# Attention in fp32: unsplit scores on halves of the rows, exponential as stationary operand, normalised by query

## The chip, the cores and the metric

The kernel runs on 1 core of one Trainium2 chip. The metric is the device time of one execution in microseconds (us); lower is better. Before the change the median of 3 runs is 2341.67 us (2341.45 to 2349.15).

## The reference, cut to what matters

Two layers work on 512 tokens (256 of context, 256 latent). Each is a feed-forward half, three token mixers side by side (S5, attention, RWKV-7), a gated merge of the three, and another feed-forward half. Attention has 8 query heads of width 64 over 2 key/value heads (4 query heads to each). Latent queries see all 512 tokens, context queries only the 256 context tokens, and the second layer needs no context output.

```python
def attend(q, k, v):
    s = jnp.einsum('bqhgd,bkhd->bhgqk', q, k).astype(F32) * (HEAD_DIM ** -0.5)
    p = jax.nn.softmax(s, axis=-1).astype(v.dtype)
    return jnp.einsum('bhgqk,bkhd->bqhgd', p, v)
...
    def merge(gate_pre, ys5, yatt, yrw):
        g_s5, g_att, g_rw = jnp.split(jax.nn.sigmoid(gate_pre), N_BRANCH, axis=-1)
        mixed = g_s5 * (ys5 @ w_br_s5) + g_att * (yatt @ w_br_att) + g_rw * (yrw @ w_br_rwkv)
        return mixed @ w_out
```

## The kernel before, in words

Most products are fp32 made of three products in the reduced type fp32r: each operand is split into a high part (a copy by ACT, L932, L921) and a low part (a subtraction, mostly on DVE, L933, L922), and `mm3` (L937 to L939) multiplies high by high, high by low and low by high. In the function `mixers` one layer's dense projections come first; then a generator `attention` and the S5 mixer `s5_main` are woven, step by step, into the issue of the program while RWKV-7 runs its 8 loops (0 to 7 in the first layer, 8 to 15 in the second). The gate products (`pg`, L937 to L939, 256 columns each, their weights `ghpg` and `glpg`) belong to no chain; they fill PE between other work. Which instruction stands where in each engine's queue is decided by the scheduler when the kernel is built: every engine then works its list strictly in order. After S5's last products (`s5g`, L747, then `s5tg` L749 and `s5o` L750) the S5 output goes through DRAM (`yd`, then `er`) in the first layer, is split (`es`, L1374 on ACT, L1375 on DVE) and multiplied with the merge weights (`pb..e`, with `ee` as weights, added up into `eg`, L1386 on DVE); remaining gates stand among and behind them; then the attention part of the merge follows and the output projection `po`.

Class `Att` does attention in units of (tp, half): tp=0 is context (256 keys, nk=2 blocks of 128), tp=1 latent (512 keys, nk=4), half picks 128 queries of each head group. The first layer has four units, the second two (tp=1). `kv` (L818) loads keys and values, normalises, transposes keys on PE (`atk`) and writes them split: high parts `kh` (ACT, L833) and low parts `kl` (DVE, L835), each on both halves of the 128 partitions; values likewise (`vh` L824, `vl` L825), with 64 columns of ones between the two heads. `q` (L836) does the same for queries (`atqs`, L848 and L849): the high part of a head stands on one half of the partitions and the low part on the other, so that one product over 128 rows holds two of the four terms.

`core` (L850) then has three stages. **Scores** (`ats`, L862 and L863): two fp32r products per head and query group, 40 row maxima by DVE (L864). **Exponential**: the maxima are transposed (`atm`) and stand in `mT`; for each of the two heads and each key block the scores are made again, transposed (`atp`, L883 and L884), with a third product (L885) that takes the maxima off; ACT makes `atP` = exp (L887) and its high part `atph` (L889), DVE the low part `atpl` (L890). **Values** (`ato`, L892 to L894): three products with the values as stationary operand and 512 columns of exponentials moving; 64 of the 128 result rows are the output of one head, the other 64 are its sums of exponentials. ACT copies both out (L895, L897), DVE takes the reciprocal of 128x512 sums (L899) and multiplies (L900), and `att_out` (L1284) hands the output on: split into the merge's operands (L1288, L1289 in the second layer), or through DRAM for tp=0. PSUM tiles come from four tags of two buffers each; `px` holds scores and `ato`, `pa` holds `atp`, `atm`, `atk` and `atq`.

Of the kernel before, what the change touches and what calls it, by code (L numbers as in the profile page):

```python
# [769 lines left out]
class Att:  # L770


    def __init__(s,K,L,pool,last):
# [44 lines left out]
    def kv(s,tp,kd):  # L818

        K=s.K; nc=K.nc; L=s.L  # L820
        kw=s.T([128,2,256],"qw",K.ATB[3]); nc.sync.dma_start(kw,kd)
        for h in range(2):
            v=kw[:,:,128+h*64:192+h*64]; vh=s.vh[:,2*tp:2*tp+2,2*h]
            nc.scalar.activation(vh,v,AF.Copy)  # L824
            nc.vector.tensor_sub(s.vl[:,2*tp:2*tp+2,2*h],v,vh.bitcast(F32))  # L825
        kr=s.heads(tp,1,kw[:,:,0:128].rearrange("p t (h d) -> p t h d",h=2),2,f"k{tp}")
# [2 lines left out]
        pf=pk.rearrange("p t c -> p (t c)"); c=slice(tp*256,tp*256+256)
        for hh in range(2):  # L830
            R=slice(hh*64,hh*64+64)
            for P in (R,slice(64-hh*64,128-hh*64)):
                nc.scalar.activation(s.kh[P,hh,c],pf[R],AF.Copy)  # L833
            for P in (R,slice(64-hh*64,128-hh*64)):
                nc.vector.tensor_sub(s.kl[P,hh,c],pf[R],s.kh[R,hh,c].bitcast(F32))  # L835
    def q(s,tp,half,qd):  # L836

        K=s.K; nc=K.nc; L=s.L; T=s.T; nm=f"{tp}{half}"
        qw=T([128,2,256],"qw",K.ATB[3]); nc.sync.dma_start(qw,qd)
# [5 lines left out]
        qs=T([128,2,4,128],"qs",K.ATQ,F32R)  # L845
        for hh in range(2):
            R=slice(hh*64,hh*64+64); Q=slice(64-hh*64,128-hh*64)
            nc.scalar.activation(qs[R,hh],pt[R],AF.Copy)  # L848
            nc.vector.tensor_sub(qs[Q,hh],pt[R],qs[R,hh].bitcast(F32))  # L849
        return qs  # L850
    def core(s,tp,half,qs,yd):
# [5 lines left out]
        m=T([128,8],"m",2)  # L857
        for h in range(2):
            for g in range(0,4,r):
                ps=K.ats([128,r,n],f"ats{nm}{h}{g}")  # L860
                for i in range(r):
# [612 lines left out]
```

## Time and profile before

| what | value |
|---|---|
| median of 3 runs | 2341.67 us (2341.45 to 2349.15) |
| profiled execution, its own time | 2342.22 us |
| span of that execution, first to last instruction | 2340.4 us |
| mean granted TensorE clock | 0.963 |
| PE busy | 2200.1 us (94%) |
| DVE busy | 1610.6 us (69%) |
| ACT busy | 967.5 us (41%) |
| POOL busy | 581.3 us (25%) |

The span is cut by hand into stretches of time in the rows below. In such a table of windows each engine has its busy time and, in brackets, its number of instructions in the stretch; PEclk is the mean granted TensorE clock as a share of full speed (1.0 is 2.4 GHz, 0.5 is 1.2 GHz). An fp32 product that isn't of the reduced type shows as two records of equal length on PE. Ends of records on PE are modelled, so the distance from start to start says what a product costs.

### The profile page before, as it was taken

To read this page: it belongs to the slowest core of one execution; us is meant where nothing else is said; L and a number is where in the kernel's file an instruction comes from. 1 tells how busy PE (TensorE), PEld (TensorE's weight loads), DVE (VectorE), ACT (ScalarE), POOL (GpSimd) and SP (SyncE) were. 2 spreads that over 40 slices of the span, in tenths; PEclk is the share of its full clock that TensorE was granted. 3 is DMA by queue.
4 is the path that set the end of the run, shared out by engine and by line. 5 is a ranking of instruction groups with operands and counts; after the bars stand their busy time and mean duration, and the time that the engine had idled before them with its cause. 6 is when DMAs were issued, how large, how long until landed. Compare 5 with 4: busy or idle time off the path is not lost.

```text
span 2340.4 us, 40316 instructions
## 1 busy us (share of the span) xinstructions
PE 2200.1 (94%) x14562; PEld 1882.2 (80%) x14562; DVE 1610.6 (69%) x3195; ACT 967.5 (41%) x2002; POOL 581.3 (25%) x712
## 2 busy tenths in 40 slices
PE   8999888989989979899999999999998988989999
PEld 5888767868789848688888888888887877878999
DVE  4896898564887769577457575546656489877655
ACT  4333333344445442443233343324434444555554
POOL 0006663221444415400000001504103145431000
PEclk9999999989999979899999999999997979999999
DMA  7574665324343624545445436536513534455664
GB/s 277 184 227 147 206 223 181 124 76 159 103 122 109 212 73 135 177 140 174 132 142 180 130 112 214 187 121 201 189 55 108 160 97 128 139 179 192 178 188 131
DMA packets 222668, 363.42 MB, mean 155 GB/s; under 512 B 54018, under 2 KB 94082, under 8 KB 221316
## 3 DMA queue, kind: packets, MB, share of 16 engines
q1 hardware_dynamic: 220308, 360.09, 48.2%
q8 instruction: 114, 1.87, 0.3%
q10 hardware_dynamic: 2160, 0.76, 0.1%
q14 instruction: 86, 0.70, 0.1%
HBM read 320.90 MB, written 39.86 MB: 154 GB/s over the span
## 4 chain that ended last, share of the span: by engine, by line
PE 59%; DVE 9%; DMA 3%; issue 3%; POOL 2%; ACT 2%; SPq 1%; ACTq 0%; DVEq 0%; POOLq 0%
PE p L938 13%; PE p L937 13%; PE p L939 13%; PE pg L939 2%; PE pg L937 2%; PE pg L938 2%; PE it L208 1%; PE po L939 1%; PE po L937 1%; PE po L938 1%; DVE s5w L705 1%; PE s5y L722 1%; DMA wrq<-w_q 1%; DVE glpg L922 0%; PE pq L938 0%
## 5 line engine op out<-in xcount | busy, mean ns | idle before, releaser
L932 ACT ACTIVATE wh<-wr 128x512 fp32r<-128x512 f32 (+1 forms) x568 | 348.7, 619 | 689.6 <-PE p L938 606.4
L933 DVE TENSOR_TENSOR wl<-wr,wh 128x512 fp32r<-128x512 f32 (+1 forms) x568 | 411.6, 728 | 298.0 <-ACT wh L932 280.0
L938 PE MATMUL p<-hlo,wh 128*128 128x512 f32 (+1 forms) x1440 | 519.1, 361 | 1.5 <-DVE hlo L1124 0.9
L939 PE MATMUL p<-hhi,wl 128*128 128x512 f32 (+1 forms) x1440 | 518.3, 360 | 0.0
L937 PE MATMUL p<-hhi,wh 128*128 128x512 f32 (+1 forms) x1440 | 514.2, 362 | 2.6 <-ACT hhi L1077 1.5
L938 PEld LDWEIGHTS p<-hlo,wh 128*128 128x128 f32 x1440 | 274.1, 190 | 43.9 <-DVE hlo L1124 1.8
L937 PEld LDWEIGHTS p<-hhi,wh 128*128 128x128 f32 x1440 | 271.7, 190 | 45.0 <-ACT hhi L1077 1.6
L939 PEld LDWEIGHTS p<-hhi,wl 128*128 128x128 f32 x1440 | 274.1, 190 | 40.8 <-issue 0.6
L1007 DVE SCALAR_TENSOR_TENSOR s<-ad,cb 128x1024 f32<-128x1024 f32 x224 | 292.2, 1306 | 4.1 <-DMA ad<-w_ada 1.1
L937 PE MATMUL p<-ghi,wh 128*128 128x512 f32 (+1 forms) x704 | 248.9, 354 | 0.0
L939 PE MATMUL p<-ghi,wl 128*128 128x512 f32 (+1 forms) x704 | 248.5, 353 | 0.0
L938 PE MATMUL p<-glo,wh 128*128 128x512 f32 (+1 forms) x704 | 248.3, 353 | 0.0
L939 PE MATMUL pg<-hhi,glpg 128*128 128x256 f32 x512 | 154.3, 303 | 7.5 <-DVE glpg L922 5.2
L937 PE MATMUL pg<-hhi,ghpg 128*128 128x256 f32 x512 | 153.1, 299 | 2.2 <-ACT ghpg L921 2.2
L938 PE MATMUL pg<-hlo,ghpg 128*128 128x256 f32 x512 | 148.8, 291 | 0.0
L937 PEld LDWEIGHTS p<-ghi,wh 128*128 128x128 f32 x704 | 133.2, 189 | 18.7 <-issue 0.6
L939 PEld LDWEIGHTS p<-ghi,wl 128*128 128x128 f32 x704 | 133.1, 189 | 18.1
L938 PEld LDWEIGHTS p<-glo,wh 128*128 128x128 f32 x704 | 133.2, 189 | 17.7
L921 ACT ACTIVATE ghpg<-wrpg 128x256 fp32r<-128x256 f32 x176 | 72.7, 415 | 127.2 <-PE pg L938 108.3
L939 PEld LDWEIGHTS pg<-hhi,glpg 128*128 128x128 f32 x512 | 100.5, 197 | 18.8 <-DVE glpg L922 8.1
L1107 POOL TENSOR_TENSOR rsf<-msf,mhalf 128x2 f32<-128x2 f32 x5 | 3.6, 712 | 426.9 <-DVE msf L1106 426.9
L937 PEld LDWEIGHTS pg<-hhi,ghpg 128*128 128x128 f32 x512 | 101.3, 198 | 8.8 <-ACT ghpg L921 5.2
(724 smaller groups left out, 4244.7 us busy)
## 6 DMA issues: line engine op xcount, KB each, us to landing
wr<-w SPq DMA_DIRECT2D x480, 256.0 KB
ad<-w_ada SPq DMA_DIRECT2D x128, 512.0 KB
wrpg<-w_g SPq DMA_DIRECT2D x96, 256.0 KB
wr<-w SPq DMA_DIRECT2D x64, 192.0 KB
s5tab<-s5tabd SPq DMA_DIRECT2D x16, 640.0 KB
s5tabd<-s5tb SPq DMA_DIRECT2D x16, 384.0 KB
wrpf<-w_f SPq DMA_DIRECT2D x24, 256.0 KB
wrq<-w_q SPq DMA_DIRECT2D x24, 256.0 KB
```

The lines of the kernel that those rows point to most:

```text
L208: nc.tensor.matmul(pi[:,c,:],BK[R,c].rearrange("p j b -> p (j b)"),s.ZL[par][R,hf,dq,c,o],start=True,stop=True)
L705: V.tensor_tensor_scan(w[:,jj,c,1:129],m,a[:,jj,c,:],initial=0.0,op0=ALU.mult,op1=ALU.add)
L722: x=hv(St[d][:,jj,c]); nc.tensor.matmul(hv(py[:,jj]),CLs[d][:,c,jj,sl],x[:,:,::-1] if d else x,start=False,stop=(d==1 and c==1))
L921: K.nc.scalar.activation(hi,raw,AF.Copy)
L932: nc.scalar.activation(hi[:,0:n],raw,AF.Copy)
L933: (nc.gpsimd if eng=='pool' or i<=K.PW else nc.vector).tensor_sub(lo[:,0:n],raw,hi[:,0:n].bitcast(F32))
L937: nc.tensor.matmul(ps,lhi,rhi,start=start,stop=False)
L938: nc.tensor.matmul(ps,lhi,rlo,start=False,stop=False)
L939: return nc.tensor.matmul(ps,llo,rhi,start=False,stop=stop).ins
L1007: nc.vector.scalar_tensor_tensor(K.junk,raw,1.0,K.cb[:,v,:],op0=ALU.mult,op1=ALU.mult,accum_out=K.M[L][:,v,ct:ct+1])
L1107: nc.gpsimd.tensor_tensor(rs[:,r],ms[:,r],K.mhalf[:,0:2],op=ALU.pow)
```

## The change

Nothing is split in attention any more; its products are plain fp32.

- `kv` loads keys and values by three transfers per call instead of one, values straight into a tile `v` whose 65th column is one. One copy by ACT (`kT`) takes the place of four copies and four subtractions. `q` has one copy by ACT in place of two copies and two subtractions.
- Scores: one product per head and group over 64 rows, the two heads on opposite halves of the rows, written one after the other in the code; head 0 goes to PSUM tag `px`, head 1 to `pa`.
- Exponential: for each key block first the product with the maxima (`sel`, L864 of the new kernel), then one over 64 rows (L865). `atph` and `atpl` are gone.
- Values: four products per head and key block (L861), with 128x128 exponentials as stationary operand and 65 columns of values and ones moving. They stand a key block behind the scores. Queries are now on the partitions, so that the sums of exponentials are one column per group: reciprocals of 128x4 (L873), a multiplication of 128x4x64 per head (L874), and four transposes by PE per unit (`atz`, L876) to bring features back onto partitions.
- `attp` has 4 buffers in place of 1, `atto` 2 in place of 1. `att_out` reads the transposed tile from PSUM; for tp=0 ACT copies it out first (`atyz`).

```diff
-            nc.scalar.activation(vh,v,AF.Copy)
-            nc.vector.tensor_sub(s.vl[:,2*tp:2*tp+2,2*h],v,vh.bitcast(F32))
...
+        for t in range(2): nc.sync.dma_start(s.v[:,2*tp+t,:,0:64],kd[:,t,128:256].rearrange("p (h d) -> p h d",h=2))
...
-                nc.scalar.activation(s.kh[P,hh,c],pf[R],AF.Copy)
...
-                nc.vector.tensor_sub(s.kl[P,hh,c],pf[R],s.kh[R,hh,c].bitcast(F32))
+        nc.scalar.activation(s.kT[:,tp*256:tp*256+256],pk.rearrange("p t c -> p (t c)"),AF.Copy)
...
+        qs=T([128,4,128],"qs",K.ATQ)
+        nc.scalar.activation(qs,pt,AF.Copy)
...
-                    nc.tensor.matmul(ps[:,i],qs[:,h,g+i],s.kh[:,h,0:n],start=True,stop=False)
-                    s.mark=nc.tensor.matmul(ps[:,i],qs[:,h,g+i],s.kl[:,h,0:n],start=False,stop=True)
...
+            pp=[(K.px,K.pa)[h]([128,r,n],f"ats{nm}{h}{g}") for h in range(2)]
+            for i in range(r):
+                for h in range(2): nc.tensor.matmul(pp[h][:,i],qs[R[h],g+i],s.kT[R[h],0:n],start=True,stop=True)
+            for h in range(2): V.tensor_reduce(m[:,h*4+g:h*4+g+r],pp[h],axis=AX.X,op=ALU.max,negate=True)
...
+        po=[K.px([128,4,65],f"ato{nm}{h}") for h in range(2)]
+        def values(k,P):
+            for g in range(4):
+                for h in range(2): nc.tensor.matmul(po[h][:,g],P[h][:,g],s.v[:,k,h],start=k==0 and g==0,stop=k==nk-1 and g==3)
+        for k in range(nk):
+            pp=[K.pa([128,4,128],f"atp{nm}{h}{k}") for h in range(2)]
+            for h in range(2): nc.tensor.matmul(pp[h],s.sel[:,h:h+1].to_broadcast([128,128]),s.mT,start=True,stop=False)
+            for h in range(2): nc.tensor.matmul(pp[h],s.kT[R[h],k*128:k*128+128],qs[R[h]].rearrange("p g n -> p (g n)"),start=False,stop=True)
+            if k: values(k-1,P)
+            P=[s.tp([128,4,128],f"P{nm}{h}{k}") for h in range(2)]
+            for h in range(2): nc.scalar.activation(P[h],pp[h],AF.Exp)
+            if k==nk//2-1: yield
+        values(nk-1,P)
+        y=s.to([128,4,2,64],f"y{nm}"); rc=T([128,8],"rc",2)
         for h in range(2):
...
-                ps=K.pa([128,4,128],f"atp{nm}{h}{k}"); kc=slice(k*128,k*128+128)
-                qf=qs[:,h].rearrange("p g n -> p (g n)")
-                nc.tensor.matmul(ps,s.kh[:,h,kc],qf,start=True,stop=False)
-                nc.tensor.matmul(ps,s.kl[:,h,kc],qf,start=False,stop=False)
-                nc.tensor.matmul(ps,s.sel[:,h:h+1].to_broadcast([128,128]),s.mT,start=False,stop=True)
-                P=s.tp([128,4,128],f"P{nm}{h}{k}")
-                nc.scalar.activation(P,ps,AF.Exp)
-                ph=T([128,4,128],"ph",K.ATP[0],F32R); pl=T([128,4,128],"pl",K.ATP[1],F32R)
-                nc.scalar.activation(ph,P,AF.Copy)
-                V.tensor_sub(pl,P,ph.bitcast(F32))
-                vh=s.vh[:,k,h:h+2].rearrange("p a d -> p (a d)")
-                nc.tensor.matmul(po,vh,ph,start=k==0,stop=False)
-                nc.tensor.matmul(po,s.vl[:,k,h:h+2].rearrange("p a d -> p (a d)"),ph,start=False,stop=False)
-                nc.tensor.matmul(po,vh,pl,start=False,stop=k==nk-1)
-            nc.scalar.activation(y[R],po[R],AF.Copy)
-            if h==0: dn=s.tt([128,4,128],f"dn{nm}")
-            nc.scalar.activation(dn[R],po[O],AF.Copy)
-            if h==0: yield
-        for g in range(0,4,K.RG): V.reciprocal(dn[:,g:g+K.RG],dn[:,g:g+K.RG])
-        V.tensor_mul(y,y,dn)
-        yd(tp,half,y)
+            V.reciprocal(rc[:,h*4:h*4+4],po[h][:,:,64])
+            V.tensor_mul(y[:,:,h],po[h][:,:,0:64],rc[:,h*4:h*4+4].unsqueeze(2).to_broadcast([128,4,64]))
+        pt=K.pa([128,4,128],f"atz{nm}")
+        for g in range(4): nc.tensor.transpose(pt[:,g],y[:,g].rearrange("p h d -> p (h d)"),K.ident)
+        yd(tp,half,pt)
```

The scheduler makes every engine's list anew, and the change moves much in `mixers` that it doesn't name. Below, a row is the line, the operation, result and operands by their names (the digits of `atp`, `ato` and `ats` are layer, tp, half, head, and key block or group), the shape that moves, and a count.

PE, first layer, unit tp=1, half=0, first and second key block, before:

```order
L885 MATMUL atp01000_7504<-atmT0_6877,atsel0_6882 128x512
L883 MATMUL atp01001_7517<-atqs0_7246,atkh0_6870 128x512
L884 MATMUL atp01001_7517<-atqs0_7246,atkl0_6871 128x512
L885 MATMUL atp01001_7517<-atmT0_6877,atsel0_6882 128x512
L939 MATMUL pg09_9172<-hhi_86,glpg094_9210 128x256
```

The same place now (L913 to L915 is `mm3` in the new kernel, L323 and L343 belong to RWKV):

```order
L913 MATMUL pg021_8536<-hhi_86,ghpg0214_8573 128x256
L864 MATMUL atp01001_7435<-atmT0_6876,atsel0_6879 128x512
L865 MATMUL atp01001_7435<-atqs0_7200,atkT0_6870 128x512
L861 MATMUL ato0100_7423<-atv0_6871,atP010000_7431 128x65 x4
L864 MATMUL atp01011_7436<-atmT0_6876,atsel0_6879 128x512
L865 MATMUL atp01011_7436<-atqs0_7200,atkT0_6870 128x512
L861 MATMUL ato0101_7424<-atv0_6871,atP010100_7432 128x65 x4
L343 MATMUL py07_6756<-XV03_6653,AM0_4070 64x64 x8
```

The 64-row products of the two heads (L865) are written side by side in the code, and stand here with values of one head and the product with the maxima between them.

PE, first layer, the end of attention and the first `s5g` products, before:

```order
L892 MATMUL ato0111_7797<-atph0_7817,atvh0_6872 128x512
L893 MATMUL ato0111_7797<-atph0_7817,atvl0_6873 128x512
L894 MATMUL ato0111_7797<-atpl0_7818,atvh0_6872 128x512
L747 MATMUL s5g00_7870<-s5g40_7795,s5tab0_7865 128x512
L747 MATMUL s5g00_7870<-s5g40_7863,s5tab0_7865 128x512
L892 MATMUL ato0111_7797<-atph0_7830,atvh0_6872 128x512
L893 MATMUL ato0111_7797<-atph0_7830,atvl0_6873 128x512
L894 MATMUL ato0111_7797<-atpl0_7831,atvh0_6872 128x512
L747 MATMUL s5g01_7878<-s5g40_7795,s5tab0_7865 128x512
L747 MATMUL s5g01_7878<-s5g40_7863,s5tab0_7865 128x512
```

The same place now, the last values of head 1 and then the transposes of the last unit with `s5g` behind them:

```order
L861 MATMUL ato0111_7616<-atv0_6871,atP011130_7687 128x65 x4
L915 MATMUL pg08_8955<-hhi_86,glpg084_8993 128x256
L913 MATMUL pg08_8955<-hhi_86,ghpg084_8992 128x256
L914 MATMUL pg08_8955<-hlo_87,ghpg084_8992 128x256
...
L876 MATMUL atz011_7704<-ident_69,aty0110_7698 128x128 x4
L747 MATMUL s5g00_7725<-s5g40_7652,s5tab0_7720 128x512
L747 MATMUL s5g00_7725<-s5g40_7718,s5tab0_7720 128x512
L913 MATMUL pg09_9027<-hhi_86,ghpg090_9030 128x256
```

Attention now ends ahead of `s5g`, and gate products stand between its last instructions and behind `s5g`, where there was none.

DVE, second layer, around S5's output (`s5o`) and the merge's first sum (`egAM`), before:

```order
L750 SCALAR_TENSOR_TENSOR s5o_20288<-s5tg_20287,s5g_20268 128x256
L1386 SCALAR_TENSOR_TENSOR egAM_20871<-egAM_20871,pb10e_20888 128x256
L1283 TENSOR_TENSOR hlo<-s5o_20288,hhi 128x256
L899 RECIPROCAL atdn_20175<-atdn_20175 128x256 x2
L1386 SCALAR_TENSOR_TENSOR egAM_20871<-egAM_20871,pb10e_20879 128x256
L1386 SCALAR_TENSOR_TENSOR egAM_20871<-egAM_20871,pb11e_20903 128x256
L922 TENSOR_TENSOR ee_20970<-ew_20969,ee_20970 128x512
L900 TENSOR_TENSOR aty_20120<-aty_20120,atdn_20175 128x512
```

The same place now:

```order
L873 RECIPROCAL atrc_20001<-ato_19902 128x4
L874 TENSOR_TENSOR aty_20000<-ato_19902,atrc_20001 128x4x64
L873 RECIPROCAL atrc_20001<-ato_19903 128x4
L874 TENSOR_TENSOR aty_20000<-ato_19903,atrc_20001 128x4x64
L1265 TENSOR_TENSOR hlo<-atz_20006,hhi 128x2x2x128
L750 SCALAR_TENSOR_TENSOR s5o_20031<-s5tg_20030,s5g_19954 128x256
L898 TENSOR_TENSOR glpo_21407<-wrpo_21404,ghpo_21406 128x256
L1259 TENSOR_TENSOR hlo<-s5o_20031,hhi 128x256
L750 SCALAR_TENSOR_TENSOR s5o_20040<-s5tg_20039,s5g_20020 128x256
```

The long reciprocals that stood between two sums of the merge are gone, and attention's output is handed on (L1265) ahead of S5's.

## Rows read from the trace of the kernel before

**Rows 1.** Windows of the first layer's mixers: us, busy time per engine, clock, DMA.

```profile
649.40:682.60 33.20, 26.55 (x303) 24.02 (x302) 31.25 (x80) 15.88 (x43) 18.48 (x20) 0.95 0.41 121
682.60:771.40 88.80, 86.79 (x1263) 79.04 (x1263) 70.04 (x131) 44.49 (x97) 44.70 (x44) 1.00 0.35 115
771.40:855.50 84.10, 74.66 (x470) 61.00 (x470) 59.00 (x103) 39.05 (x77) 24.09 (x24) 0.92 0.45 151
855.50:871.70 16.20, 7.73 (x19) 4.34 (x20) 10.89 (x14) 8.62 (x14) 0.90 (x5) 0.80 0.38 132
871.70:907.40 35.70, 33.16 (x169) 26.80 (x168) 33.91 (x116) 7.41 (x13) 15.90 (x11) 0.95 0.35 107
907.40:945.60 38.20, 37.11 (x214) 31.37 (x213) 29.95 (x98) 10.80 (x19) 29.77 (x57) 1.00 0.41 125
```

**Rows 2.** Windows of the second layer's mixers, columns PE, PEld, DVE, ACT, POOL likewise.

```profile
1935.70:1988.50 52.80, 45.09 (x745) 39.78 (x744) 48.33 (x107) 25.89 (x63) 28.16 (x33) 0.92 0.44 133
1988.50:2044.50 56.00, 55.77 (x593) 48.98 (x585) 44.99 (x88) 30.68 (x73) 25.59 (x29) 1.00 0.44 139
2044.50:2079.60 35.10, 28.72 (x219) 23.79 (x219) 27.26 (x58) 21.43 (x50) 13.44 (x15) 1.00 0.67 200
2079.60:2093.40 13.80, 9.91 (x49) 8.38 (x49) 10.91 (x18) 6.01 (x12) 1.46 (x2) 0.78 0.29 96
```

**Rows 3.** What ACT sat idle for ahead of the exponentials (L887): us, times.

```profile
  DVE atpl L890: 18.3, 22
```

**Rows 4.** Waits of PE, 820 to 880 us: line, releaser, total, times, longest.

```profile
PE pb00e L937 <- ACT es L1374: 8.0, 1, 8.0
```

**Rows 5.** Timeline of PE, a wait in the second layer's tail.

```profile
2088.78 0.58 PE L937 MATMUL pb11e<-hhi,ee 128*128 128x256 f32 x1 [3.49 <-DVE egAM L1386]
```

**Rows 6.** Timeline of PE: a gate product, then fp32r products of 512 columns.

```profile
813.79 0.28 PE L938 MATMUL pg<-hlo,ghpg 128*128 128x256 f32 x1
813.90 0.40 PE L892 MATMUL ato<-atph,atvh 128*128 128x512 f32 x1
814.14 0.39 PE L893 MATMUL ato<-atph,atvl 128*128 128x512 f32 x1
```

**Rows 7.** Timeline of PE: two plain fp32 products of 512 columns, four records.

```profile
858.05 1.88 PE L747 MATMUL s5g<-s5g,s5tab 128*128 128x512 f32 x4
...
859.99 0.39 PE L893 MATMUL ato<-atph,atvl 128*128 128x512 f32 x1
```

**Rows 8.** Timeline of PE: plain fp32 products, stationary 128x128, 64 columns moving.

```profile
2060.41 1.06 PE L722 MATMUL s5y<-s5S,s5CLm 128*128 128x64 f32 x8
2061.30 0.39 PE L717 MATMUL s5y<-s5U,s5TTm 128*128 128x64 f32 x2
```

**Rows 9.** Timeline of PE: fp32 products over 64 rows, opposite halves, side by side.

```profile
476.59 0.48 PE L151 MATMUL pw<-wal,rwwa 64*128 64x256 f32 x1
476.60 0.48 PE L152 MATMUL pa<-wal,rwwa 64*128 64x256 f32 x1
...
477.22 0.50 PE L937 MATMUL pf<-hhi,ghpf 128*128 128x512 f32 x1
```

**Rows 10.** Timeline of PE: one such product alone among gate products.

```profile
599.71 0.28 PE L938 MATMUL pg<-hlo,ghpg 128*128 128x256 f32 x1
599.92 0.70 PE L152 MATMUL pa<-wal,rwwa 64*128 64x256 f32 x2
600.54 0.39 PE L939 MATMUL pg<-hhi,glpg 128*128 128x256 f32 x1
```

**Rows 11.** Lines L890, L899 over the whole span: duration ns min/median/max, first and last start.

```profile
L890 DVE TENSOR_TENSOR atpl<-atP,atph x40: 673/693/1675, 707.5 to 2082.0; 128x512 fp32r<-128x512 f32 x40
L899 DVE RECIPROCAL atdn<-atdn x8: 1695/2547/3352, 726.6 to 2086.8; 128x512 f32<-128x512 f32 x4, 128x256 f32<-128x256 f32 x4
```

**Rows 12.** Chain that ended last, 649 to 715 us: start, us, what.

```profile
669.46 0.41 DVE atkl L835
693.18 0.68 DVE atqs L849
```

More of the change, by code (lines that the diff above doesn't have):

```diff
@@ L820, in kv @@
         K=s.K; nc=K.nc; L=s.L
[L821 to L826 removed]
+        kw=s.T([128,2,128],"kw"); nc.sync.dma_start(kw,kd[:,:,0:128])
+        for t in range(2): nc.sync.dma_start(s.v[:,2*tp+t,:,0:64],kd[:,t,128:256].rearrange("p (h d) -> p h d",h=2))
+        kr=s.heads(tp,1,kw.rearrange("p t (h d) -> p t h d",h=2),2,f"k{tp}")
         pk=K.pa([128,2,128],f"atk{L}{tp}")
         for t in range(2): nc.tensor.transpose(pk[:,t],kr[:,t].rearrange("p h d -> p (h d)"),K.ident)
[L829 to L832, printed above, removed]
[L833 to L835 removed]
+        nc.scalar.activation(s.kT[:,tp*256:tp*256+256],pk.rearrange("p t c -> p (t c)"),AF.Copy)
     def q(s,tp,half,qd):
         K=s.K; nc=K.nc; L=s.L; T=s.T; nm=f"{tp}{half}"
[L839 removed]
+        qw=T([128,2,256],"qw",2); nc.sync.dma_start(qw,qd)
         qr=s.heads(tp,0,qw.rearrange("p t (h d) -> p t h d",h=4),4,f"q{nm}")
@@ L856, in core @@
         nk=2 if tp==0 else 4; nm=f"{L}{tp}{half}"; r=4//nk; n=nk*128
[L857 to L861, printed above, removed]
-                    nc.tensor.matmul(ps[:,i],qs[:,h,g+i],s.kh[:,h,0:n],start=True,stop=False)
-                    s.mark=nc.tensor.matmul(ps[:,i],qs[:,h,g+i],s.kl[:,h,0:n],start=False,stop=True)
-                V.tensor_reduce(m[:,h*4+g:h*4+g+r],ps,axis=AX.X,op=ALU.max,negate=True)
+        m=T([128,8],"m",2); R=(slice(0,64),slice(64,128))
+        for g in range(0,4,r):
+            pp=[(K.px,K.pa)[h]([128,r,n],f"ats{nm}{h}{g}") for h in range(2)]
+            for i in range(r):
+                for h in range(2): nc.tensor.matmul(pp[h][:,i],qs[R[h],g+i],s.kT[R[h],0:n],start=True,stop=True)
+            for h in range(2): V.tensor_reduce(m[:,h*4+g:h*4+g+r],pp[h],axis=AX.X,op=ALU.max,negate=True)
         yield
@@ L1283, in ysplit, with att_out @@
             nc.vector.tensor_sub(K.hlo[:,a:b,0:256],v,K.hhi[:,a:b,0:256].bitcast(F32))
-        def att_out(tp,half,py):
+        def att_out(at,tp,half,py):
             k=2+half*2
@@ L1293, in att_out @@
                 nc.vector.tensor_sub(w(1),v,w(0).bitcast(F32)); return
+            y=at.to([128,4,128],f"yz{tp}{half}"); nc.scalar.activation(y,py,AF.Copy)
             for i in range(2):
-                nc.sync.dma_start(K.yd[:,k:k+2,tp*256+i*128:tp*256+i*128+128],py[:,i*2:i*2+2])
+                nc.sync.dma_start(K.yd[:,k:k+2,tp*256+i*128:tp*256+i*128+128],y[:,i*2:i*2+2])
         W=rwkv_load(K,L)
@@ L1354, in attention @@
                 nq=at.q(*un[i+1],K.qd[un[i+1][0],un[i+1][1]]) if i+1<len(un) else None
-                yield from at.core(*u,qs,att_out); qs=nq
+                yield from at.core(*u,qs,lambda *a: att_out(at,*a)); qs=nq
                 yield
```

26 lines of the change are left out of this document (7 added, 19 removed).

## The prediction

> **What bounds the kernel now.** I read the windows first, stage by stage, because PE's 94% over the span is a mean over stages with different limits. In the first layer's mixers [rows 1] the first stretch is DVE's: 31.25 us busy of 33.2, PE 26.55. The second is PE's: 86.79 of 88.8, full clock. The third (84.1 us) belongs to nobody: PE 74.66, DVE 59.00, ACT 39.05, clock 0.92. There the gate products run out and attention walks alone, exponential, high part, low part, next exponential: ACT sat idle 18.3 us in 22 places ahead of exponentials, each time for DVE's low part [rows 3]. The fourth stretch is a gap, PE 7.73 of 16.2, since the merge waits 8.0 us for S5's split output [rows 4]. The fifth is DVE's again (33.91 of 35.7), the sixth PE's (37.11 of 38.2). The second layer [rows 2] repeats this on a smaller scale: DVE's stretch (48.33 of 52.8), PE's (55.77 of 56.0), one that is neither's (PE 28.72 of 35.1) and a tail of 13.8 us at clock 0.78, in which PE stands 3.49 us for a sum of the merge on DVE [rows 5], queued behind attention's long reciprocals.
>
> **What the change costs on PE.** Prices, from start to start: a gate product 0.11 to 0.12 us, an fp32r product of 512 columns 0.24 [rows 6] (0.23 to 0.235 in longer series, used below). A plain fp32 product is two records; four of them and one fp32r product take 1.94 us [rows 7], so a record costs (1.94 - 0.23) / 4 = 0.43 and the product 0.85, for 256 columns half of it. With 128x128 stationary and 64 columns eight records take 0.89 us, 0.111 each [rows 8]: few columns save nothing below that, and I take 0.111 for 65 columns too.
>
> Over 64 rows, two products on opposite halves run side by side when they are neighbours: four records of two products take 0.63 us for 256 columns [rows 9]. Alone among other products, one of them takes 0.62 us [rows 10] where two records would be 0.43 plus the ordinary step of 0.12 from the gate ahead of it: 599.71 to 600.54 is 0.83, less 0.12, less 0.43, so coming in and going out cost 0.28. The new order puts only 5 of the 44 possible pairs side by side; the others are parted, by gates, or by values and the product with the maxima. I count 64 such detours.
>
> Removed: 48 score pairs (32 of 512 columns, 16 of 256) and 40 times 3 products for the exponential and 3 for values, 32 x 0.47 + 16 x 0.24 + 240 x 0.235 = 75 us. Added: 32 x 0.85 + 16 x 0.43 + 40 x 0.85 = 68, less 4 for the five pairs, plus 64 x 0.28 = 18 for detours; 40 x 0.235 = 9 for the maxima; 160 values x 0.222 = 36; 24 transposes x 0.111 = 3. Sum 130. **PE gets 55 us more work**, 33 in the first layer and 22 in the second.
>
> The row-tile rule of the Trainium skill ("TensorE: Matmul & The Clock Gate", Part 3, Packing small matmuls) says that products on distinct row groups run concurrently; [rows 9] agree for neighbours. The same section says that products start and end strictly in program order, by which a parted pair gains nothing; [rows 10] agree.
>
> **What it saves on DVE.** 40 low parts at 0.69 to 0.8 and 8 reciprocals, 2.5 on average [rows 11], are 48 to 52 us; with the splits of keys, queries and values 70 us leave DVE's list for 4 that come. That counts only where DVE or attention's own chain ends the stage. ACT loses copies, which bound nothing by themselves.
>
> **First layer.** First two stretches: PE grows 1.8 us in the first, which DVE's bound hides, and 5.2 in the second, which nothing hides. Against it the key and query low parts that lie on the chain go: four of 0.42 and two of 0.68 [rows 12], 3.1 us. Net +2. Third stretch, to the first `s5g`: the alternation of ACT and DVE is gone, values stand a key block behind, and gates stretch to its end. What is left is PE's list, counted through the new order at the prices above: 73.9 us in place of 64.4, plus 2 for its waits, 76 for 84.1: -8. It gets there by moving 125 to 144 gate products behind `s5g`, 15 to 17 us of PE. There they lie beneath two things: the 8.0 us wait, of which I take 3 as gained (the other 5 only hold work that was elsewhere), and DVE's fifth stretch, where PE has room but where the gates bring splits for DVE, by the order 4.4 us, of which I take +3. By the list PE goes from 72 to 88 us over these last three stretches, which last 90: it fits, barely. First layer: +2 - 8 - 3 + 3 = -6.
>
> **Second layer.** DVE's stretch loses four low parts of keys (0.42) and one of queries (0.67) on the chain, -2; PE's stretch pays its growth of 4.6 in full; together +2. The third stretch has PE at 25.7 us by the list and 39.4 after: with 2 of waits 41.4 for 35.1, +6. The tail loses the reciprocals and the last alternation: its 9.9 us of PE are stretched by the clock, and what must still run there at full clock is about 5 us, so 13.8 becomes 5, -9. Second layer: -1.
>
> What I cost at nothing: values come by small-piece transfers, three issues on SP per `kv` call for one, but the first values are used after maxima and scores, tens of us behind the keys. Transposes and the copy `atyz` ahead of the transfer to `yd` in the first layer: its reader (`ea`) stands behind eight rounds of the merge.
>
> **Sum:** -7 on the profiled execution's 2342.2 us, which lies 0.55 above the median: **2335**. Bounds of the unknown terms (third stretch 0 to -10, moved gates -3 to +8, tail -4 to -9, loops -2 to +7) give 2327 to 2349.
>
> **Rivals.** A measurement of this kernel can tell about 0.5% (11.7 us) from no change.
>
> *DVE's relief counts in full.* In DVE's two stretches the splits that leave add to 5.7 and 6.7 us where I credit 5.3 for both, and the order moves further splits of gates out of them; the stretch of the merge then doesn't grow either. That is 7 more in the loops and 3 to 4 in the merge: about 2324. For it: DVE at 92 to 94% busy [rows 1, 2]. Against it: those loops are a serial solve by DVE and PE in turn, with transfers in its chain.
>
> *The change does what it says of halves:* parted products over 64 rows overlap as well. Then the 88 products cost about half, PE grows by 20 in place of 55, and some 21 of these 35 us lie in stretches that PE bounds: 2314. Against it: [rows 10].
>
> By the row-tile rule of the Trainium skill, read without its sentence on order, this is what would happen; no parted pair of the trace shows it.
>
> *Slower: PE's extra work is paid.* The moved gates find no room behind `s5g`, since PE's list there has 88 us for 90 and any wait breaks that. Of 55 us, covered is only what attention's own chain left idle: 19.7 in the third stretch (84.1 less 64.4), 8.0 of the wait, 9 of the tail, 36.7 in all. Then +18.5: 2360. It decides at whether the fifth stretch stays near 36 us or grows to 50. For it: PE is busy 94% and this is the largest term. Against it: DVE bounds that stretch.
>
> **How the numbers follow.** Forecast 0.45 (own range 2327 to 2349), relief 0.22, overlap 0.06, slower 0.27. Faster by over 0.5% (below 2330): 0.08 of the forecast, 0.17 of the relief, the overlap: 0.31. Slower (above 2353): 0.01 and 0.22: 0.23. Within: 0.46. The range takes in the overlap and most of the slower case, 2312 to 2362, leaving out some 0.18.
>
> **What would show it.** Right: no alternation ahead of `s5g`; gates up to it at full clock; the fourth stretch's wait short; L865 0.85 us or more, apart from its partner; the merge of the first layer near 36 us; the second layer's tail without DVE's gap. Wrong: the merge at 50 us, PE waiting inside the third stretch (then the chain of values and maxima bounds it), or 64-row products of both heads starting within 0.02 us of each other all through.

## The result, and the profile after

The median of 20 executions is **2355.43 us** (2339.3 to 2366.5), that of the kernel before 2341.56 us (2332.28 to 2349.15) in as many: a ratio of **1.0062**, interval 1.0045 to 1.0079. The change makes the kernel slower by 0.6%, 14 us. The forecast, 2335, was within 0.5% of no change on the other side; the time lies in the range 2312 to 2362, in its slower part, near the slower rival's 2360. The profiled execution has a span of 2359.9 us (2361.73 us in all, 6 above the median), 19.5 more than the one of before. PE is busy 2247.5 us in place of 2200.1, DVE 1556.3 in place of 1610.6, ACT 924.9 in place of 967.5.

To see where the 19.5 us come from, both traces are cut at the same events: the solve's copy at the head of a loop (L305), the first `s5g` product, the first and sixteenth sum of the merge (`eg`), and the first (first layer) or last (second layer) product of `po` with `ghpo` as weights.

| stretch | before | after | moved | forecast |
|---|---|---|---|---|
| first layer, loop 0 to loop 7 | 123.5 | 120.4 | -3.1 | +2 |
| to `s5g` | 78.4 | 75.7 | -2.7 | -8 |
| to the merge's first sum | 18.6 | 21.1 | +2.5 | -3 |
| to its sixteenth | 33.3 | 37.6 | +4.3 | +3 |
| to `po` | 38.2 | 37.8 | -0.4 | 0 |
| `po` to the second layer's loop 8 | 994.3 | 988.2 | -6.1 | 0 |
| second layer, loop 8 to loop 11 | 50.3 | 54.8 | +4.5 | both: +2 |
| loop 11 to loop 15 | 57.9 | 64.1 | +6.2 | |
| to `s5g` | 30.3 | 45.8 | +15.5 | +6 |
| to the last of `po` | 55.4 | 52.5 | -2.9 | -9 |

(1.0 us ahead of the first stretch and 0.7 behind the last make up the rest.) The first layer comes out at +0.6, the second at +23.3. The windows of the changed kernel over these stretches, columns as in [rows 1, 2]:

```profile
654.60:775.00 120.40, 115.29 (x1508) 93.56 (x1510) 86.28 (x194) 43.48 (x103) 55.54 (x58) 1.00 0.34 106
775.00:850.70 75.70, 75.70 (x480) 54.39 (x477) 34.24 (x71) 23.36 (x50) 16.76 (x18) 1.00 0.42 133
850.70:871.80 21.10, 19.99 (x130) 16.61 (x129) 13.33 (x40) 10.89 (x22) 6.89 (x12) 1.00 0.60 197
871.80:909.40 37.60, 34.38 (x202) 29.32 (x201) 36.57 (x131) 8.55 (x16) 17.29 (x15) 1.00 0.41 126
...
1935.40:1990.20 54.80, 47.88 (x714) 39.06 (x713) 37.91 (x90) 21.24 (x50) 28.12 (x32) 0.82 0.39 116
1990.20:2054.30 64.10, 63.40 (x571) 45.48 (x572) 36.46 (x77) 20.18 (x50) 19.14 (x23) 0.94 0.27 87
2054.30:2100.10 45.80, 43.63 (x288) 32.27 (x283) 27.51 (x59) 18.64 (x43) 13.93 (x16) 0.93 0.58 174
2100.10:2152.60 52.50, 48.17 (x362) 45.38 (x361) 39.63 (x82) 26.12 (x56) 14.88 (x18) 0.97 0.62 204
```

Five of these stretches in the kernel before, cut at the same events:

```profile
855.50:874.10 18.60, 10.13 (x25) 6.22 (x26) 12.23 (x17) 9.13 (x14) 2.24 (x6) 0.76 0.36 123
...
1939.90:1990.20 50.30, 43.22 (x741) 38.11 (x742) 46.09 (x100) 23.67 (x57) 26.53 (x29) 0.96 0.40 119
1990.20:2048.10 57.90, 56.07 (x601) 49.33 (x600) 46.79 (x94) 30.36 (x73) 24.83 (x29) 1.00 0.44 140
2048.10:2078.40 30.30, 26.05 (x183) 21.70 (x181) 22.59 (x46) 20.78 (x50) 12.75 (x14) 1.00 0.71 210
2078.40:2133.80 55.40, 48.61 (x350) 45.13 (x351) 44.20 (x88) 27.53 (x57) 14.54 (x16) 0.94 0.56 188
```

Read the clock first, the third column from the end. In the first layer it is 1.00 throughout, where before it was 0.8 to 0.95 in places [rows 1]: gates fill what attention's chain left idle. In the second layer it is 0.82 in loops 8 to 11, where the kernel before has 0.96, and DVE, which bounded that stretch before (46.09 of 50.3), is at 37.91 of 54.8: the bound has gone over to PE. Weighted with PE's busy time in windows of 1 us (busy time times the missing share of the clock), low clock costs PE 18.0 us in the second layer's stretches after and 4.3 before; in the first layer's 0.0 and 10.6. Over the whole span the two come out alike, 69.8 us after and 69.7 before.

The timeline of PE in the second layer shows where:

```profile
1964.94 1.98 PE L845 MATMUL ats<-atkT,atqs 64*128 64x512 f32 x4
...
1975.12 0.66 PE L831 MATMUL atq<-ident,atqnq 128*128 128x128 f32 x4 [2.05 <-POOL atqnq L812]
...
1977.68 0.42 PE L913 MATMUL pg<-hhi,ghpg 128*128 128x256 f32 x1
1977.89 0.42 PE L914 MATMUL pg<-hlo,ghpg 128*128 128x256 f32 x1
...
1981.15 3.78 PE L845 MATMUL ats<-atkT,atqs 64*128 64x512 f32 x4
...
1989.77 3.78 PE L845 MATMUL ats<-atkT,atqs 64*128 64x512 f32 x4
```

Four records of scores take 1.98 us at 2.4 GHz and 3.78 at 1.2. PE waited 2.05 us for the query's normalisation, then gate products stand 0.21 us apart in place of 0.12, and it stays so to about 1997 us although PE is busy 100% of the time in between. The question for the experiments is what of the 14 us is PE's work, above all that of the 64-row products (theory A), and what is this low clock (theory B).

### The profile page after: what moved, and what is told of

It reads as the page before. It is cut to its first block, busy times and chain, and to the rows that moved or that the text cites. A ratio compares the mean times of both kernels' runs of the same rounds, so it can differ in the third digit from the quotient of the medians.

```text
span 2359.9 us, 40561 instructions
## 1 busy us (share of the span) xinstructions
PE 2247.5 (95%) x14786; PEld 1895.0 (80%) x14786; DVE 1556.3 (66%) x3125; ACT 924.9 (39%) x1914; POOL 571.9 (24%) x714
## 4 chain that ended last, share of the span: by engine, by line
PE 64%; DVE 7%; DMA 2%; POOL 2%; issue 2%; ACT 1%; SPq 0%; ACTq 0%; POOLq 0%; DVEq 0%
PE p L914 13%; PE p L913 13%; PE p L915 13%; PE pg L915 2%; PE pg L913 2%; PE pg L914 2%; PE ato L861 2%; PE ats L845 2%; PE atp L865 2%; PE po L913 1%; PE po L915 1%; PE it L208 1%; PE po L914 1%; PE s5y L722 1%; PE atp L864 0%
## 5 line engine op out<-in xcount | busy, mean ns | idle before, releaser
L915 PE MATMUL p<-hhi,wl 128*128 128x512 f32 (+1 forms) x1440 | 520.1, 362 | 0.0
L913 PE MATMUL p<-hhi,wh 128*128 128x512 f32 (+1 forms) x1440 | 514.8, 362 | 2.6 <-ACT hhi L1053 1.5
L913 PEld LDWEIGHTS p<-hhi,wh 128*128 128x128 f32 x1440 | 273.1, 191 | 45.0 <-ACT hhi L1053 2.1
L915 PEld LDWEIGHTS p<-hhi,wl 128*128 128x128 f32 x1440 | 274.8, 191 | 40.5 <-issue 0.6
L913 PE MATMUL p<-ghi,wh 128*128 128x512 f32 (+1 forms) x704 | 249.2, 355 | 0.0
L915 PE MATMUL p<-ghi,wl 128*128 128x512 f32 (+1 forms) x704 | 248.9, 354 | 0.0
L915 PE MATMUL pg<-hhi,glpg 128*128 128x256 f32 x512 | 159.8, 314 | 8.7 <-DVE glpg L898 4.7
L913 PE MATMUL pg<-hhi,ghpg 128*128 128x256 f32 x512 | 157.1, 307 | 3.3 <-ACT ghpg L897 3.2
L913 PEld LDWEIGHTS p<-ghi,wh 128*128 128x128 f32 x704 | 133.4, 190 | 18.6 <-issue 0.6
L915 PEld LDWEIGHTS p<-ghi,wl 128*128 128x128 f32 x704 | 133.2, 189 | 18.0
L915 PEld LDWEIGHTS pg<-hhi,glpg 128*128 128x128 f32 x512 | 103.8, 203 | 24.3 <-DVE glpg L898 7.1
L913 PEld LDWEIGHTS pg<-hhi,ghpg 128*128 128x128 f32 x512 | 103.9, 203 | 19.8 <-issue 11.3
```

The costliest lines, as they stand in the source:

```text
L913: nc.tensor.matmul(ps,lhi,rhi,start=start,stop=False)
L915: return nc.tensor.matmul(ps,llo,rhi,start=False,stop=stop).ins
```

## The experiments

Each was timed beside the kernel before on its own chip, whose median was 2340.4 to 2342.8 us in these series; e1, e3, e4 and e6 ran 6 times, the others 12. Every edit but those of e8 and e9 also lets the scheduler make the order of the engines anew, so that a difference holds that too: by the operands' names some 660 of PE's 14786 records stand elsewhere in e2 than in the changed kernel. Zeros for padding, and the small products of e5, change nothing of what is computed.

**e1 and e5: the pairs side by side.** e1 wraps each pair, of the scores and of the exponential, in a section that the scheduler keeps whole:

```diff
+                with K.tc.tile_critical():
+                    for h in range(2): nc.tensor.matmul(pp[h][:,i],qs[R[h],g+i],s.kT[R[h],0:n],start=True,stop=True)
```

> The changed kernel with every pair of 64-row products (scores and exponential) kept side by side on PE, 44 pairs in place of 5. Theory A (PE's work is paid nearly one for one, and the parted products are most of it): 88 products fall from 82 us to 44 pairs at about 1.0 us, so PE loses 35 to 39 us and the time falls to 2318 to 2330 us. Theory B (what is lost is the clock: PE fell to 1.2 GHz for 20 us of the second layer, and half-filled rows keep it there): the spell stays, and the time falls only by the pairs outside it, to 2340 or above.

Measured: 2492.83 us, ratio 1.0638 (1.0613 to 1.0663). The time decides nothing between the theories: such a section first waits for other engines and transfers that it has no business with. PE's waits in it:

```profile
PE ats L846 <- DMA ew<-w_br: 6.5, 2, 3.5
PE ats L846 <- POOL glpg L900: 5.0, 1, 5.0
```

Score products waiting for a transfer of merge weights have no reason in the data. PE waits 44 times ahead of pairs, 73 us in all, these and others together; and the mean granted clock is 0.927 in place of 0.966, which weighted as above takes 146.0 us of PE's time in place of 69.8. e5 gets the neighbours by edges of order alone:

```diff
+            d=nc.tensor.matmul(pp[1][:,0,0:2],K.ident,K.ident[:,0:2],start=True,stop=True)
+            with K.tc.issue_after(d.ins):
...
+            d=[nc.tensor.matmul(pp[h],s.sel[:,h:h+1].to_broadcast([128,128]),s.mT,start=True,stop=False) for h in range(2)]
+            with K.tc.issue_after(d[1].ins):
```

> The changed kernel with the 64-row products of the two heads kept next to each other by order alone (a 2-column product reserves the second head's score tile, and the first head's product is issued behind it, or behind the second head's product with the maxima): 42 of 44 pairs side by side, where the sections of the first try made PE wait for other engines. Theory A (PE's added work is paid, and parted 64-row products are most of it): PE loses about 35 us less some 4 for the 24 small products; the time falls by 25 to 30 from the changed kernel's 2355, to 2325 to 2330. Theory B (the low clock in the second layer is what costs, and 64-row products keep it low): even pairs are half as long but the spell stays, 2335 to 2345.

Measured: 2345.42 us, ratio to before 1.0023 (1.0008 to 1.0038): 10 us less than the changed kernel. First the price of a product over 64 rows and 512 columns, parted in the changed kernel, then two as a pair in e5:

```profile
2093.09 0.40 PE L864 MATMUL atp<-atmT,atsel 128*128 128x512 f32 x1
2093.41 1.12 PE L865 MATMUL atp<-atqs,atkT 64*128 64x512 f32 x2
2094.46 1.11 PE L861 MATMUL ato<-atv,atP 128*128 128x65 f32 x8
```

```profile
2006.94 0.39 PE L866 MATMUL atp<-atmT,atsel 128*128 128x512 f32 x1
2007.26 1.13 PE L868 MATMUL atp<-atqs,atkT 64*128 64x512 f32 x4
2008.32 0.69 PE L303 MATMUL p<-XV,ZL 128*64 128x64 f32 x16
```

From the product with the maxima to what comes behind: 2093.09 to 2094.46 less 0.23 is 1.14 us for one product alone (0.85 + 0.28 = 1.13 was forecast), 2006.94 to 2008.32 less 0.23 is 1.15 us for two together. So neighbours are free, as the Trainium skill ("TensorE: Matmul & The Clock Gate", Part 3, Packing small matmuls) has it for distinct row groups. PE is busy 27 us less (2220.3), near the 31 to 35 that were expected, but the time falls by 10: PE's idle time rises from 112 to 129 us, and a spell at 1.2 GHz from 1970 to 1990 us is still there. Where the idle time comes from is not shown; attention's own products wait 2.5 us in all. The time is at B's edge (2345), not at A's 2330. Here 27 us of work taken off PE paid back 10.

**e2, e6, e7: full rows.** Queries padded with zeros on the other half of the rows, so that scores, exponential, or both are products over 128 rows. No two of them stand on opposite halves any more, and each costs 0.86 us (e8: 2054.00 to 2054.86 from start to start), where a parted one over 64 rows costs 1.14:

```diff
-        qs=T([128,4,128],"qs",K.ATQ)
-        nc.scalar.activation(qs,pt,AF.Copy)
+        qs=T([128,2,4,128],"qs",K.ATQ)
+        for hh in range(2):
+            R=slice(hh*64,hh*64+64); Q=slice(64-hh*64,128-hh*64)
+            nc.gpsimd.memset(qs[Q,hh],0.0); nc.scalar.activation(qs[R,hh],pt[R],AF.Copy)
...
-                for h in range(2): nc.tensor.matmul(pp[h][:,i],qs[R[h],g+i],s.kT[R[h],0:n],start=True,stop=True)
+                for h in range(2): nc.tensor.matmul(pp[h][:,i],qs[:,h,g+i],s.kT[:,0:n],start=True,stop=True)
...
-            for h in range(2): nc.tensor.matmul(pp[h],s.kT[R[h],k*128:k*128+128],qs[R[h]].rearrange("p g n -> p (g n)"),start=False,stop=True)
+            for h in range(2): nc.tensor.matmul(pp[h],s.kT[:,k*128:k*128+128],qs[:,h].rearrange("p g n -> p (g n)"),start=False,stop=True)
```

(This is e2. Of the two products e6 pads the first, of the scores, and e7 the second, of the exponential.)

> The changed kernel with queries padded by zeros to 128 rows, so that no product is over 64 rows and none can pair. Theory A: a product keeps its 0.85 us and loses only the 0.28 us of going in and out, 64 times, -18 us: about 2338. Theory B (half-filled rows keep the clock low): the granted clock in the second layer's loops is back near 1.0 and the time falls by 10 us more, to about 2328.

> The changed kernel with zero-padded 128-row products for the scores only; the exponential's stay over 64 rows. Theory A: 29 detours of 0.28 us go, -8: 2347. Theory B: the spell at 1.2 GHz in loops 10 and 11 of the second layer lies over eight score products, so it shrinks to a few us, -8 and up to -12 more: 2335 to 2340, clock there 0.8 or higher.

> The changed kernel with zero-padded 128-row products for the exponential only; the scores stay over 64 rows. Theory A: 35 detours of 0.28 us go, -10: 2345. Theory B: the scores are what stands in the spell of loops 10 and 11, so the spell stays as long as in the changed kernel, and the time is 2345 with a wide scatter from run to run.

Measured: both padded (e2) 2336.91, ratio 0.9977 (0.9963 to 0.9991), 12 executions from 2332 to 2342. Exponential alone padded (e7) 2340.33, ratio 1.0006 (0.9992 to 1.0021), from 2339 to 2346. Scores alone padded (e6) 2359.37, ratio 1.0080 (1.0060 to 1.0099). e2 is at A's number to 1 us, with 18.5 us off, yet with the second layer's loss to the clock back at 6.3 us, which is B's sign. e6 and e7 hit neither: I had looked for the trouble in the scores, where the profiled execution showed it (four products, eight records, not the eight products that I wrote), and the kernel in which only the exponential's products are over 64 rows is the slow one. In e6 the spell is not gone, it lies elsewhere and is 50 us long. These are its windows of 10 us, columns as before:

```profile
2040.00:2050.00 10.00, 7.91 (x40) 5.26 (x39) 8.62 (x19) 3.91 (x10) 5.52 (x6) 0.83 0.81 244
2050.00:2060.00 10.00, 10.00 (x28) 6.08 (x27) 4.33 (x7) 2.63 (x5) 4.84 (x6) 0.50 0.25 82
2060.00:2070.00 10.00, 10.00 (x38) 7.81 (x37) 0.85 (x2) 2.10 (x4) 0.00 (x0) 0.50 0.00 1
2070.00:2080.00 10.00, 10.00 (x34) 7.09 (x32) 4.79 (x10) 4.10 (x9) 0.73 (x1) 0.50 0.44 134
2080.00:2090.00 10.00, 10.00 (x28) 5.84 (x26) 2.50 (x5) 2.85 (x6) 0.00 (x0) 0.50 0.40 121
2090.00:2100.00 10.00, 10.00 (x51) 9.28 (x51) 2.05 (x6) 3.03 (x8) 2.63 (x4) 0.61 0.11 32
```

PE is full in every window but the first, and at half its clock in four of them. The stretch holds the last unit's exponentials and values, with gates between. That gave the decisive pair of runs.

**e8 and e9: eight products.** e8 is e6 with the eight exponential products of the very last unit over 128 rows; e9 is e2 with those eight over 64 rows. In each, every engine's order is that of the kernel it comes from, row for row. The edit of e8 against e6:

```diff
-            for h in range(2): nc.tensor.matmul(pp[h],s.kT[R[h],k*128:k*128+128],qs[R[h],h].rearrange("p g n -> p (g n)"),start=False,stop=True)
+            for h in range(2): nc.tensor.matmul(pp[h],s.kT[X[h],k*128:k*128+128],qs[X[h],h].rearrange("p g n -> p (g n)"),start=False,stop=True)
```

(X is all 128 rows for the second layer's second unit and R elsewhere in e8; the other way round in e9.)

> The kernel with padded scores and 64-row exponentials (e6_full_scores), in which the 8 products of the exponential of the very last unit are padded to 128 rows too; every engine's order of instructions is the same, only these 8 products differ. Theory A (a 64-row product costs its 0.28 us of going in and out, no more): 8 x 0.28 = 2 us less, 2357. Theory B (64-row products keep a low clock low): the spell of 50 us at 1.2 GHz that lies over this unit ends within some 10 us, so some 20 us go: 2335 to 2342.

> The reverse: the kernel with all products padded to 128 rows (e2_full_rows), in which the 8 products of the exponential of the very last unit go over 64 rows; every engine's order is the same. Theory A: 2 us more, 2339. Theory B: the clock, which falls here to 1.2 GHz at about 2050 us for a short time, stays low over this unit in some or all executions: 2340 to 2358, with a wider scatter than the 10 us of the padded kernel.

Measured: e8 2335.34 us, ratio 0.9982 (0.9969 to 0.9995): **24 us less than e6 for eight products**. e9 2356.44 us, ratio 1.0063 (1.0036 to 1.0089): **19.5 us more than e2 for the same eight**. A's price for them is 2 us. (The pairs were timed on different chips; by their ratios to the kernel before it is 0.98% and 0.86%, 23 and 20 us.) e9's 12 executions stand in two groups: two at 2333.6 and 2334.8 us with a mean clock of 0.974 and 0.971, ten from 2353.0 to 2368.2 with 0.957 to 0.966. The windows of e8 over the same stretch as e6 above:

```profile
2040.00:2050.00 10.00, 7.91 (x55) 6.59 (x54) 9.60 (x22) 4.44 (x12) 4.54 (x6) 1.00 0.80 236
2050.00:2060.00 10.00, 10.00 (x69) 8.33 (x68) 7.12 (x12) 4.66 (x10) 6.25 (x6) 1.00 0.37 112
2060.00:2070.00 10.00, 10.00 (x64) 7.91 (x63) 5.49 (x12) 6.43 (x15) 0.78 (x1) 1.00 0.83 243
2070.00:2080.00 10.00, 9.27 (x69) 8.49 (x67) 4.74 (x13) 5.75 (x15) 3.61 (x5) 1.00 0.33 104
```

And PE's timeline at the head of the stretch, e6 and then e8:

```profile
2044.15 0.38 PE L917 MATMUL pg<-hhi,glpg 128*128 128x256 f32 x1 [1.24 <-DVE glpg L900]
...
2046.48 0.47 PE L917 MATMUL pg<-hhi,glpg 128*128 128x256 f32 x1 [0.65 <-DVE glpg L900]
...
2047.95 2.07 PE L867 MATMUL atp<-atqs,atkT 64*128 64x512 f32 x2
2049.96 0.58 PE L917 MATMUL pg<-hhi,glpg 128*128 128x256 f32 x1
```

```profile
2045.14 0.39 PE L917 MATMUL pg<-hhi,glpg 128*128 128x256 f32 x1 [1.24 <-DVE glpg L900]
...
2047.46 0.39 PE L917 MATMUL pg<-hhi,glpg 128*128 128x256 f32 x1 [0.64 <-DVE glpg L900]
...
2048.42 1.02 PE L867 MATMUL atp<-atqs,atkT 128*128 128x512 f32 x2
```

The same waits for split gate weights, 1.24 and 0.65 us, stand ahead in both. In e6 the clock is down when the first of the eight 64-row products starts and comes back 7 us behind the last of them; one such product then takes 2.07 us. In e8 it is not down at all in the profiled execution. These are windows of e2, where it is down for a short time, and then one of e9:

```profile
2050.00:2060.00 10.00, 8.79 (x40) 6.40 (x41) 8.69 (x19) 4.76 (x13) 6.56 (x7) 0.83 0.57 178
2060.00:2070.00 10.00, 10.00 (x69) 8.33 (x69) 5.04 (x11) 5.53 (x11) 2.08 (x3) 1.00 0.54 157
```

```profile
2050.00:2060.00 10.00, 10.00 (x61) 7.14 (x61) 6.07 (x12) 4.19 (x10) 2.72 (x4) 1.00 0.41 125
```

The profiled execution of e9 is its fastest (2333.6 us): there the same eight 64-row products run at full clock. So they don't bring the clock down; but where it was down ahead of them, in e6, it stayed down for 50 us, and without them, in e2, it was back within 4. The ten slower executions of e9 fit this with their lower mean clock, but none of them left a profile. Theory B holds for this unit. The other 32 products of the exponential are over 64 rows in e8, and it is as fast as e2: how much of such products' price the time shows depends on where they stand.

**e3 and e4: the two halves of the change alone.** e3 keeps the kernel before's split scores (three fp32r products over 128 rows) and takes the new values and normalisation; e4 takes the new 64-row scores and keeps the old values.

```diff
+            for h in range(2):
+                kc=slice(k*128,k*128+128); qf=qs[:,h].rearrange("p g n -> p (g n)")
+                nc.tensor.matmul(pp[h],s.kh[:,h,kc],qf,start=True,stop=False)
+                nc.tensor.matmul(pp[h],s.kl[:,h,kc],qf,start=False,stop=False)
+                nc.tensor.matmul(pp[h],s.sel[:,h:h+1].to_broadcast([128,128]),s.mT,start=False,stop=True)
...
-            for h in range(2): nc.tensor.matmul(pp[h],s.kT[R[h],k*128:k*128+128],qs[R[h]].rearrange("p g n -> p (g n)"),start=False,stop=True)
```

> The kernel before with the new values and normalisation only (scores and exponential's scores stay split in three fp32r products). PE grows by 36 + 3 - 28 = 11 us, DVE loses 48 to 52 us, and the alternation of ACT and DVE is gone. Theory A: the 20 us that attention's chain left idle pay for 11 us of PE: 2328 to 2338, faster than both. Theory B: the same, with the clock as high as before in the second layer's loops. If it is at 2350 or above, it is the values and not the scores that cost.

> The kernel before with the new 64-row scores only (values and normalisation as before, split exponentials). PE grows by 82 + 9 - 46 = 45 us, DVE loses only about 18 us, and the alternation of ACT and DVE stays. Theory A: slower than the changed kernel, about 2365 to 2380. Theory B: the time depends on low-clock spells in the second layer's loops; with them 2365 or more, without them near 2350.

Measured: e3 **2328.27 us, ratio 0.9938 (0.9918 to 0.9958), faster than both kernels**. (To fit into memory it has one buffer in place of two for the query's load and for attention's output.) e4 2393.33, ratio 1.0225 (1.0189 to 1.0261), above the 2365 to 2380 of A and within B's "2365 or more". e3's third stretches, first and second layer:

```profile
782.30:849.10 66.80, 66.80 (x534) 62.84 (x530) 35.04 (x73) 27.27 (x57) 20.22 (x22) 1.00 0.52 164
...
2031.90:2068.20 36.30, 33.23 (x256) 29.81 (x253) 23.89 (x57) 17.54 (x41) 13.27 (x15) 0.95 0.68 205
```

In the first layer that is 66.8 us where the kernel before takes 78.4 and the changed one 75.7: here is the gain that I expected from ending the alternation of ACT and DVE. In the second it is 36.3, between 30.3 and 45.8. e4, with the alternation and the 64-row products, has 92.1 us there and a spell like the others in its second layer:

```profile
2000.00:2010.00 10.00, 10.00 (x80) 5.34 (x79) 2.79 (x5) 1.59 (x3) 0.00 (x0) 0.50 0.05 16
2010.00:2020.00 10.00, 10.00 (x101) 7.05 (x100) 5.20 (x11) 1.22 (x3) 0.00 (x0) 0.50 0.13 41
```

**PE's work, the clock and the idle time apart.** PE's busy time, less what low clock takes of it (weighted as above, over the whole span), is PE's work at full clock. Each row is one profiled execution, in us:

| kernel | PE busy | lost to low clock | work at full clock | PE idle |
|---|---|---|---|---|
| before | 2200.1 | 69.7 | 2130.4 | 140.3 |
| changed | 2247.5 | 69.8 | 2177.7 | 112.4 |
| e2, both padded | 2220.6 | 59.4 | 2161.2 | 118.8 |
| e7, exponential padded | 2223.7 | 51.7 | 2172.0 | 114.8 |
| e6, scores padded | 2246.6 | 76.8 | 2169.8 | 111.1 |
| e8, e6 with eight more padded | 2227.5 | 59.8 | 2167.7 | 105.3 |
| e1, pairs kept whole | 2284.4 | 146.0 | 2138.4 | 213.2 |
| e5, pairs by order | 2220.3 | 68.5 | 2151.8 | 129.2 |
| e3, values only | 2197.6 | 60.1 | 2137.5 | 130.8 |
| e4, scores only | 2261.8 | 77.2 | 2184.6 | 131.5 |

Against the kernel before, the changed one has 47.3 us more work, no more loss to the clock, and 27.9 us less idle time: that makes the 19.5 us. The medians of the mean granted clock say the same, 0.968 over the 20 executions of the changed kernel, 0.966 over 63 of the kernel before, 0.969 over the 12 of e2. So what slows the changed kernel as a whole is PE's work (theory A), less the idle time that it takes up: e2 takes 16.5 us of work off it (A had 18) and is 18.5 faster at nearly the same clock. Pairs take 39 (e1) and 26 us (e5) off the work, but idle time takes their place, and in e1 low clock too. e6 and e8 differ by 2.1 us of work, A's 2, and by 17.0 of loss to the clock: between these two, and between e2 and e9 (median clock 0.969 and 0.962), it is theory B.

## Why the prediction was wrong

**Which step failed.** The sum set 55 us of added PE work against 62 us that were to be freed. PE's work at full clock grew by 47.3, and what paid for it is PE's idle time, which fell by only 27.9. Four terms hold the error: the second layer's loops (+2, measured +10.7), its third stretch (+6, measured +15.5), the wait in the first layer (-3, measured +2.5) and the tail (-9, measured -2.9). Together they miss 30 us; the other stretches give 3 of them back.

**The second layer's terms were priced at 2.4 GHz.** The counted prices held: a parted 64-row product 1.14 us for 1.13, a pair 1.15, eight records of values (four products) 0.92 us for 0.89. But in loops 8 to 15 low clock takes 13.3 us of PE's time in the profiled execution, before 1.8, and in the third stretch 3.1, before 0.0: 14.6 of the 18.2 us that these two terms miss. e8 and e9 show that eight 64-row products can make a difference of 20 to 24 us by the clock. For the spell of 1977 to 1997 that cause isn't shown, since RWKV's products over 32 rows (L271, L281) stand in it beside the scores. No rival had this: I read the clock of the kernel before as a result of idle time only, so that a PE with more work could only have a better one. That is what the first layer did: 10.6 us of loss are gone, and PE's idle time there fell from 29.2 to 10.8 us. But the trace of the kernel before has the contrary too, just ahead of the second layer's loops:

```profile
1912.00:1914.00 2.00, 2.00 (x15) 2.00 (x14) 1.96 (x4) 0.29 (x1) 0.00 (x0) 0.50 0.32 96
1914.00:1916.00 2.00, 2.00 (x9) 1.61 (x8) 1.97 (x4) 0.41 (x1) 1.04 (x1) 0.50 0.57 162
1916.00:1918.00 2.00, 2.00 (x130) 1.88 (x130) 0.40 (x1) 0.01 (x1) 0.72 (x1) 0.50 0.78 242
```

PE is busy all the time and at half its clock from 1910 to 1922 us. Of its records between 1912 and 1918 16 are of RWKV's products over 64 rows (`it`, L208) and 128 of products over 32 rows (`pS`, L263).

**The scatter is for the most part the clock's.** The 20 executions go from 2339.3 us at a mean clock of 0.976 to 2366.5 at 0.965. Span times clock is 2281 us in the first (2337.5 x 0.976) and 2282 in the last (2364.7 x 0.965): the same work at another clock. Over all 20 it lies between 2274 and 2291 us, where the times differ by 27.

**Term by term.** The first layer up to `s5g` was forecast at -6 and measured -5.8, with the two terms shared out differently. *"The 8.0 us wait, of which I take 3 as gained"* failed: the stretch became 2.5 us longer. Gates fill it (PE 19.99 us of 21.1, before 10.13 of 18.6), but it ends with S5's output through DRAM, and gates now also stand between the two halves of `s5g` (second `s5o` 6.6 us behind the first product in place of 5.2). Filling this wait didn't shorten it. *DVE's growth in the merge*, +3, was measured +4.3, with DVE busy 36.57 us in place of 32.57: the mechanism was right. *The loops of the second layer*, +2, measured +10.7: there the spell of 1977 to 1997 lies. *The third stretch*, +6, measured +15.5: PE is busy 43.63 us there in place of 26.05, 17.6 more, where the list had 13.7 and some 3 come from the low clock of 2070 to 2076 us; and by these events there were only 4 us of idle to take up, where I had counted on 7. *The tail*, -9, measured -2.9 up to the end of the stretch: the long reciprocals are gone, but PE is busy 48.17 us there, before 48.61, so that only idle time went (6.8 to 4.3 us). The 6.1 us less between the layers I had at zero: low clock takes 27.0 us of PE's time there in place of 32.4, which is most of it; whether every execution has that isn't shown. One sum of the prediction doesn't hold by itself: its bounds of the unknown terms, added at their worst to the third stretch's +6, give +17, which is 2359 and not 2349.

**The rivals.** "PE's extra work is paid" comes closest, and not by its number alone: the work less the idle time that it takes up is what the two profiled executions show, 47.3 less 27.9 for its 55 less 36.7. That both its parts were 8 to 9 us too large, so that the difference still came out, is luck. Its place was wrong: it was to show at the first layer's merge growing from 36 to 50 us, which grew to 37.6. The relief of DVE is there in the second layer's loops, as DVE's busy share shows (37.91 of 54.8 us), but PE took over the bound; and the merge, which that rival had as not growing, grew by 4.3. "Parted products overlap" is refuted by 1.14 us for one.

**What stays open.** Why the clock fell in e6's and not in e8's profiled execution behind the same waits, and why in the changed kernel one spell over such products (2070 to 2076 us) ended after 6 us and another went on for 20. In e6's spell no product over 64 rows stands from 2062.4 to 2072.6 us (values, S5's products and transposes do), and the clock stays low there too. In e7, where only the scores are over 64 rows, no spell in the second layer's loops is longer than 8 us; whether scores can hold one by themselves was not tried.

## What to carry to other kernels

When a change swaps products over the full rows for products over half of them, price them at both clocks: look for every place where PE waits shortly before them, and put a run with zero-padded operands beside it, which costs a few lines. Half-row products gained here only as neighbours, and the scheduler kept 5 of 44 pairs so. Take PE's work, the clock's loss and the idle time apart before saying which of them a change paid with. And take the change apart before judging it: here one half (values with the exponential as stationary operand, normalised by query) is worth -14 us, and the other, on top of it, costs 27.

## What the runs showed that was not expected

- With the order of every engine the same, eight products of 512 columns over 64 in place of 128 rows changed the median by 19.5 and 24 us, in e6's profiled execution with PE busy throughout and its granted clock at 0.50 for about 50 us; over 128 rows the clock was at 1.00 in the same place (e8) or back there within 4 us (e2).
- One kernel's executions can stand in two groups 18 us apart (2334.8 and 2353.0), with a mean clock of 0.971 and above in one and 0.966 and below in the other.
- In the kernel before, PE was busy all the time at half its clock from 1910 to 1922 us, over products of 64 and 32 rows among others.
- A section that the scheduler keeps whole cost 137 us over the changed kernel (2492.8 for 2355.4), by waits for engines and transfers, some of which its two products don't depend on, and a granted clock of 0.927 in place of 0.966.
